# The conditioning of the first block on TensorE: plain fp32 products in four column strips in place of dot products on VectorE

## The chip, the cores and the metric

The kernel runs on one core of a Trainium2 chip, as one program with one launch. The metric is the device time of one execution in microseconds (us). The kernel before was timed three times: 2343.14 us in the median, 2342.88 to 2343.78. The profile shows one more execution of the same program. The engines are named as in the profile: PE is TensorE's matrix products, PEld its weight loads, DVE is VectorE, ACT is ScalarE, POOL is GpSimd, SP is SyncE, whose queue issues nearly all DMAs.

## The reference, cut to what matters

Two transformer blocks work on 256 tokens of width 1024. The change lies in the first of them, up to its FFN:

```python
c_act = silu(c)                                  # one row of 1024
mod = c_act @ ada_w + ada_b                      # [1024] x [1024, 6144]
sh1, sc1, g1, sh2, sc2, g2 = split(mod, 6)       # six rows of 1024
h = rmsnorm(x, mix_norm_pre) * (1 + sc1) + sh1
y = windowed_gqa_sink(h, w_qkv, w_o, ...)        # 16 q heads, 4 kv heads, 256 tokens
x = x + g1 * rmsnorm(y, mix_norm_post)
h = rmsnorm(x, ffn_norm_pre) * (1 + sc2) + sh2
y = swiglu(h, ffn_w_in, ffn_w_out)
x = x + g2 * rmsnorm(y, ffn_norm_post)
```

`mod` is called the conditioning here. It is a vector of 6144 numbers, each a dot product of 1024 terms, kept on the chip as a tile `mod1` of 128 partitions x 48 columns: column j holds outputs 128j to 128j+127. Attention needs sh1 and sc1 (columns 0 to 15) before anything else, g1 (16 to 23) at its end, sh2 and sc2 (24 to 39) ahead of the FFN, g2 (40 to 47) at the end of the FFN. The rest of the program (the FFN, the second block with its expert layers) is the same work before and after.

## The kernel before, in words

All dense weights are fp32 and are multiplied as sums of fp32r parts: `split` rounds a weight tile on ACT to `hi` (L199) and takes `lo` = raw - `hi` on DVE or on POOL (L200; the word "pool" in the weights' plan says which). A product is then three fp32r matmuls: hi x hi, hi x lo, lo x hi. Small products (attention scores, values, transposes) are plain fp32.

**The front (to the first q tile).** SP issues the loads in the order of the code: x, constants, the row c, the bias table's inputs, then the weights of the conditioning's first 16 columns (16 tiles of 512 KB, two in one DMA) with the four k/v weight slabs in between. ACT and DVE normalize x and PE transposes it into four PSUM banks (`T_half`, L389). Then comes a loop over four slabs (`kv_prep`, `kv_T`, `kv_mm`). For each, DVE makes four columns of the conditioning (`ada`, L318: a 128x1024 tile of weights times the broadcast row silu(c), summed along the row into one column of `mod1`), ACT and DVE turn two banks of transposed x into the parts `hTh` and `hTl` (L412, L417, L419), and PE multiplies them with the slab (L675 to L677). A small product (L638) selects the rows of the bias table; DVE masks it (L682), ACT's queue writes it to DRAM, and SP reads it back.

**The attention loop (`for u in range(16 + 6)`).** A step u is one half of a pair of heads. PE makes the scores of u (L732), the transposes of u-3 (L766), the values of u-4 (L779) and, in every second step, the next q tile (24 fp32r products, L223 to L225); from u = 16 on, one tile of the output projection each. DVE adds the bias and finds the maximum (L735, L738, L740), and normalizes (L755 to L757); ACT takes the exponentials (L747). A list `pending` holds generators whose pieces are spread over the loop by `pump`: here `ada` for columns 16 to 39, one or two dot products of DVE in a step. Of the 16 splits of q and output weights, 12 take their `lo` on POOL.

**Behind the loop.** The gate's row is made on PE (`row_pe`, L348), the last two tiles of the output projection follow (`gemm_tail`), `drain()` finishes what is left of the conditioning on DVE, and then DVE and ACT normalize, add to x, normalize again, PE transposes, and the FFN begins.

All engines run their own instructions strictly in the order of the code; there is no scheduler. Eight PSUM banks, five `raw` tiles for loaded weights and seven `big` tiles come from rotating pools.

Of the kernel before, what the change touches and what calls it, by code (L numbers as in the profile page):

```python
# [19 lines left out]
P = 128  # L20
# [18 lines left out]
NCOLS = 253  # L39
# [41 lines left out]
def _plan(t):  # L81

    p = [(("q", j), t["att_q"][j], "pool") for j in range(8)]
    p += [(("o", k), t["att_o"][k], ("big", "big pool")[k % 2] if k >= 8 - O_TAIL else "pool" if k % 2 else None) for k in range(8)]
# [27 lines left out]
O_TAIL = 2  # L112
# [12 lines left out]
def tile_two_blocks(ctx: ExitStack, tc: tile.TileContext, t: dict, taps=None):  # L125
# [176 lines left out]
    def ada(w, row, mod, bcol, chunks, group=8, loaded=None, also=None):  # L302
# [4 lines left out]
        for i, j in enumerate(chunks):  # L307
# [14 lines left out]
            if j % group == group - 1:  # L322
                s = slice(j - group + 1, j + 1)
                for o, c, m in todo:
                    vec.tensor_tensor(out=m[:, s], in0=m[:, s], in1=cols[:, bcol + s.start:bcol + s.stop], op=OP.add)
            yield
# [276 lines left out]
    for s in range(2):  # L603
        dma(out=X[:, s, :], in_=t["x"][s * P:s * P + P, :])
    dma(out=kst[:, 0:256], in_=t["kst"][:, 0:256])
    dma(out=crow, in_=t["c"].partition_broadcast(P))
# [3 lines left out]
    dma(out=cols[:, 0:C_AB2], in_=t["cols"][:, 0:C_AB2])  # L610
    order, early, kvw = [], [], big()
    for q in range(4):
        a = big().rearrange("p (c k) -> p c k", c=4)
        for i, j in enumerate((8 + 2 * q, 2 * q)):
            dma(out=a[:, 2 * i:2 * i + 2, :], in_=t["ada1"][j:j + 2].rearrange("c p k -> p c k"))
            order += [j, j + 1]
        early += [a[:, i, :] for i in range(4)]
        dma(out=kvw[:, q * 1024:q * 1024 + 1024], in_=t["att_kv"][q])
    W.load_to(W.used + 2)
    dma(out=sink, in_=t["sink"].partition_broadcast(P))  # L620
    mhalf = const.tile([P, 2], F32, name="mhalf")
    vec.memset(mhalf, -0.5)
    mod1 = mods[0]
    first = ada(t["ada1"], crow, mod1, C_AB1, order, 2, early)
# [4 lines left out]
    cand_c = kst[:, K_CAND:K_CAND + 32]  # L629
    bs = T_banks()  # L630
    for hf in range(2):
        rms_half(X, N, hf)
        T_half(bs, N, hf)
        if hf == 0:
            silu_row(crow)

    b = mm([P, 512])
    pe.matmul(b[0:16, :], lhsT=rb, rhs=oh[0:32, :], start=True, stop=True)  # L638
# [11 lines left out]
    def kv_prep(k2):  # L650

        j = k2 * 2
        kvs[k2] = split(kvw[:, k2 * 1024:k2 * 1024 + 1024], "pool")
        for i in range(4):
            if i == 2 and k2:
                kv_T(k2 - 1, None, vec)
                kv_mm(k2 - 1)
            next(first)
# [1133 lines left out]
```

## Time and profile before

| | |
|---|---|
| time, median of 3 runs | 2343.14 us (2342.88 to 2343.78) |
| the profiled execution's own time | 2341.82 us |
| its span | 2340.0 us |
| PE busy in the span | 2231.0 us (95%) |
| DVE busy | 1723.9 us (74%) |
| ACT busy | 1159.4 us (50%) |
| POOL busy | 223.7 us (10%) |
| DMA, mean | 227 GB/s |

The shares are means over the whole program; the change touches its first 167 us alone, up to the FFN's first product. So the rows further down are of that stretch, and of two later places where PE does what the kernel before does not do in it. A product's end is modelled in the profile: products overlap, and what one costs in a stream is read from the distance of two starts, not from its duration. "Idle before" in brackets is the engine's wait and what ended it.

### The profile page before, as it was taken

The numbers are of one execution on the slowest core, as the hardware profiler recorded it, in microseconds if no ns is written. First come the engines' busy times: TensorE is split into PE (matmuls) and PEld (weight loads), VectorE is DVE, ScalarE is ACT, GpSimd is POOL, SyncE is SP. The second block draws the span as 40 slices with busy tenths as digits, with TensorE's granted clock in tenths as the row PEclk, the third lists the DMA queues.
The fourth block names the chain that finished last, engine by engine and source line by source line (L and its number), as shares of the span: only waits on it lengthen the run. The fifth ranks groups of instructions, "written<-read, shape, count | busy, mean of one in ns | idle before, by whom it ended". The sixth has DMA issues, their size and how long they took to land. (4 is left out here: it accounts for less than half of the span.)

```text
span 2340.0 us, 36878 instructions
## 1 busy us (share of the span) xinstructions
PE 2231.0 (95%) x14334; PEld 1979.0 (85%) x14334; DVE 1723.9 (74%) x2870; ACT 1159.4 (50%) x1693; POOL 223.7 (10%) x142
## 2 busy tenths in 40 slices
PE   5979899997999999999999999999999999999998
PEld 4668888875799999998988887889999998988886
DVE  5989977727689778776787667769877746566666
ACT  4663344348555544534444445554455544444443
POOL 2234410111220000000000001230000000000001
PEclk8989999999999999999999999999999999999999
DMA  8566686730555677898899776545577777777774
GB/s 333 198 205 228 240 274 223 264 98 28 189 164 191 211 260 261 271 323 274 288 301 304 244 247 225 191 161 181 192 240 241 245 225 231 214 240 240 245 245 153
DMA packets 205023, 531.61 MB, mean 227 GB/s; under 512 B 16336, under 2 KB 84464, under 8 KB 204720
## 3 DMA queue, kind: packets, MB, share of 16 engines
q1 hardware_dynamic: 195600, 495.67, 63.6%
q10 hardware_dynamic: 9248, 33.59, 4.4%
q8 instruction: 112, 1.84, 0.3%
q14 instruction: 63, 0.52, 0.1%
HBM read 492.45 MB, written 36.75 MB: 226 GB/s over the span
## 5 line engine op out<-in xcount | busy, mean ns | idle before, releaser
L200 DVE TENSOR_TENSOR lo<-raw,hi 128x1024 fp32r<-128x1024 f32 x621 | 769.2, 1241 | 443.8 <-ACT hi L199 442.3
L199 ACT ACTIVATE hi<-raw 128x1024 fp32r<-128x1024 f32 x668 | 705.3, 1059 | 777.0 <-PE mm L244 359.7
L225 PE MATMUL mm<-hTh,lo 128*128 128x256 f32 x2592 | 739.9, 285 | 21.9 <-POOL lo L200 14.6
L223 PE MATMUL mm<-hTh,hi 128*128 128x256 f32 x2592 | 748.4, 289 | 0.7 <-ACT hTh L417 0.7
L224 PE MATMUL mm<-hTl,hi 128*128 128x256 f32 x2592 | 736.5, 284 | 0.2 <-DVE hTl L419 0.2
L225 PEld LDWEIGHTS mm<-hTh,lo 128*128 128x128 f32 x2592 | 500.1, 193 | 29.0 <-POOL lo L200 18.1
L223 PEld LDWEIGHTS mm<-hTh,hi 128*128 128x128 f32 x2592 | 500.4, 193 | 4.3 <-issue 3.0
L224 PEld LDWEIGHTS mm<-hTl,hi 128*128 128x128 f32 x2592 | 500.7, 193 | 0.7 <-POOL hTl L419 0.5
L242 PE MATMUL mm<-lo,s 128*128 128x512 f32 x992 | 305.9, 389 | 2.6 <-DVE lo L200 2.6
L240 PE MATMUL mm<-hi,s 128*128 128x512 f32 x992 | 305.6, 389 | 0.0
L244 PE MATMUL mm<-hi,s 128*128 128x512 f32 x992 | 305.5, 389 | 0.0
L200 POOL TENSOR_TENSOR lo<-raw,hi 128x1024 fp32r<-128x1024 f32 x47 | 123.0, 2619 | 1057.1 <-ACT hi L199 1035.8
L242 PEld LDWEIGHTS mm<-lo,s 128*128 128x128 f32 x992 | 186.0, 188 | 42.3 <-DVE lo L200 3.7
L244 PEld LDWEIGHTS mm<-hi,s 128*128 128x128 f32 x992 | 186.1, 188 | 39.0 <-DVE s L200 0.3
L240 PEld LDWEIGHTS mm<-hi,s 128*128 128x128 f32 x992 | 185.8, 188 | 38.4
L1424 ACT ACTIVATE t<-mm 128x512 f32<-128x512 f32 x128 | 75.7, 592 | 88.5 <-DMA gspill<-t 43.2
L318 DVE SCALAR_TENSOR_TENSOR raw<-raw,t 128x1024 f32<-128x1024 f32 x84 | 104.7, 1246 | 19.9 <-DMA raw<-in_ada_dram 15.4
L427 POOL TENSOR_TENSOR sm<-sm,mhalf 128x1 f32<-128x1 f32 (+1 forms) x18 | 11.5, 640 | 863.7 <-DVE sm L426 863.6
L1406 DVE TENSOR_TENSOR t<-t,pk 128x1024 f16<-128x1024 f16 x128 | 88.6, 692 | 4.5
L1417 PE MATMUL mm<-t 128*128 128x128 f16 x1024 | 79.7, 220 | 11.2 <-DVE t L1406 11.2
L1403 DVE TENSOR_TENSOR t<-pk,iota 128x1024 f16<-128x1024 f16 x128 | 87.7, 685 | 0.7 <-PE mm L1417 0.7
L318 DVE SCALAR_TENSOR_TENSOR raw<-raw,big 128x1024 f32<-128x1024 f32 x40 | 81.1, 2029 | 8.5 <-DMA raw<-in_ada_dram 7.7
(284 smaller groups left out, 2507.7 us busy)
## 6 DMA issues: line engine op xcount, KB each, us to landing
raw<-in_u_dram SPq DMA_DIRECT2D x256, 512.0 KB, 4.2
raw<-in_v_dram SPq DMA_DIRECT2D x256, 512.0 KB, 4.0
raw<-in_ada_dram SPq DMA_DIRECT2D x124, 512.0 KB, 4.6
gspill<-t ACTq DMA_DIRECT2D x64, 512.0 KB, 3.3
t<-gspill SPq DMA_DIRECT2D x64, 512.0 KB, 5.5
raw<-in_ffn_in_dram SPq DMA_DIRECT2D x44, 512.0 KB, 4.4
raw<-in_ab_in_dram SPq DMA_DIRECT2D x32, 512.0 KB, 4.8
raw<-in_ffn_out_dram SPq DMA_DIRECT2D x22, 512.0 KB, 4.7
```

The source lines that it names most:

```text
L199: act.activation(out=hi, in_=src, func=AF.Copy)
L200: (eng or vec).tensor_tensor(out=lo, in0=src, in1=hi.bitcast(F32), op=OP.subtract)
L223: pe.matmul(out, lhsT=sh, rhs=mh, start=(i == 0), stop=False)
L224: pe.matmul(out, lhsT=sh, rhs=ml, start=False, stop=False)
L225: pe.matmul(out, lhsT=sl, rhs=mh, start=False, stop=(i == n - 1))
L240: pe.matmul(o[c], lhsT=sh[:, tk], rhs=wh[:, cs[c]], start=first, stop=False)
L242: pe.matmul(o[c], lhsT=sh[:, tk], rhs=wl[:, cs[c]], start=False, stop=False)
L244: pe.matmul(o[c], lhsT=sl[:, tk], rhs=wh[:, cs[c]], start=False, stop=last)
L318: vec.scalar_tensor_tensor(out=o, in0=r, scalar=1.0, in1=c, op0=OP.mult, op1=OP.mult, accum_out=m[:, j:j + 1])
L1403: vec.tensor_tensor(out=o12, in0=pk[:, 0].rearrange("p a q n -> p (a q) n").unsqueeze(2).to_broadcast([P, 4, P, 2]), in1=iota2.unsqueeze(1 ...
L1406: vec.tensor_tensor(out=o[:, 1024:2048].rearrange("p (a q i n) -> p a q i n", q=2, i=P, n=2), in0=o1.to_broadcast([P, 2, 2, P, 2]), in1=pk ...
L1417: pe.matmul(b[:, n, :], lhsT=o[:, 0, a, 1, :, m], rhs=o[:, 1, a, q, :, m], start=q == 0, stop=q == 1)
```

## The change

`ada_pe` takes the place of `ada` for columns 0 to 39 of the first block's conditioning. The weights are laid out anew in DRAM (`ada1n`: ten groups of 512 outputs, each in four pieces of 128 partitions x 1024). A piece holds two slices of 128 inputs (z = 0, 1), each for 512 outputs, and the outputs in two halves of 256 (h = 0, 1). For each of the four pairs (z, h) PE does one plain fp32 product of 256 columns: the stationary operand is one column of silu(c) (a new 8-column part of `cols`) repeated 32 times, and the output goes to 32 partitions of one PSUM bank, which start at 64z + 32h. These are the four column strips. After four pieces ACT copies the bank to SBUF, and two small products with a 128x2 tile `strips` (which adds the strips of z = 0 and z = 1) turn the rows into four columns of `mod1`; DVE adds the bias. So a group is five steps of the generator. The groups 2, 0, 3, 1 are done in the front (10 steps, then 2 and 1 between the k/v products, then 7), the groups 4 to 9 in the attention loop, where `pump(1)` now stands twice in each step. The four k/v slabs are treated in two halves of two, all `lo` parts up to the last output tile are on DVE, the bias table's product and its masking stand ahead of the normalization of x, and the row c is loaded and activated later. Columns 40 to 47 stay dot products on DVE.

```diff
@@ _plan
-    p = [(("q", j), t["att_q"][j], "pool") for j in range(8)]
-    p += [(("o", k), t["att_o"][k], ("big", "big pool")[k % 2] if k >= 8 - O_TAIL else "pool" if k % 2 else None) for k in range(8)]
+    p = [(("q", j), t["att_q"][j], None) for j in range(8)]
+    p += [(("o", k), t["att_o"][k], "big" if k >= 8 - O_TAIL else None) for k in range(8)]
@@ new, behind ada
+    def ada_pe(groups, pieces=None):
+        todo = [(g, q) for g in groups for q in range(4)]
+        nxt = None if pieces else load(t["ada1n"][todo[0]])
+        for i, (g, q) in enumerate(todo):
+            if pieces:
+                r = pieces[i]
+            else:
+                r = nxt
+                nxt = load(t["ada1n"][todo[i + 1]]) if i + 1 < len(todo) else None
+            r = r.rearrange("p (z h n) -> p z h n", z=2, h=2)
+            if q == 0:
+                b = mm([P, 512])
+            for z in range(2):
+                c = cols[:, C_CC + 2 * q + z:C_CC + 2 * q + z + 1].to_broadcast([P, 32])
+                for h in range(2):
+                    o = 64 * z + 32 * h
+                    pe.matmul(b[o:o + 32, 0:256], lhsT=c, rhs=r[:, z, h, :], start=q == 0, stop=q == 3)
+            if q < 3:
+                yield
+                continue
+            f = s1(256)
+            act.activation(out=f, in_=b[:, 0:256], func=AF.Copy)
+            yield
+            o = b[:, 256:260].rearrange("p (h a) -> p h a", a=2)
+            for a in range(2):
+                pe.matmul(o[:, :, a], lhsT=f[:, a * P:a * P + P], rhs=strips, start=True, stop=True)
+            vec.tensor_tensor(out=mods[0][:, g * 4:g * 4 + 4], in0=b[:, 256:260],
+                              in1=cols[:, C_AB1 + g * 4:C_AB1 + g * 4 + 4], op=OP.add)
+            yield
@@ the front: loads, then the bias table ahead of the normalization of x
-    dma(out=crow, in_=t["c"].partition_broadcast(P))
+    dma(out=cols[:, 0:C_AB2], in_=t["cols"][:, 0:C_AB2])
+    dma(out=cols[:, C_CC:NCOLS], in_=t["cols"][:, C_CC:NCOLS])
...
+    early, kvw = [], big()
+    for i, g in enumerate((2, 0, 3, 1)):
         a = big().rearrange("p (c k) -> p c k", c=4)
+        for q in range(4):
+            dma(out=a[:, q, :], in_=t["ada1n"][g, q])
+            early.append(a[:, q, :])
+        if i % 2:
+            for q in range(i - 1, i + 1):
+                dma(out=kvw[:, q * 1024:q * 1024 + 1024], in_=t["att_kv"][q])
...
-    first = ada(t["ada1"], crow, mod1, C_AB1, order, 2, early)
+    act.activation(out=cols[:, C_CC:NCOLS], in_=cols[:, C_CC:NCOLS], func=AF.Silu)
...
+    strips = const.tile([P, 2], F32, name="strips")
+    vec.tensor_tensor(out=strips, in0=ident[:, 0:64:32], in1=ident[:, 64:128:32], op=OP.add)
+    first = ada_pe((2, 0, 3, 1), early)
     bs = T_banks()
+    b = mm([P, 512])
+    pe.matmul(b[0:16, :], lhsT=rb, rhs=oh[0:32, :], start=True, stop=True)
+    vec.tensor_tensor(out=msk[0:16, :], in0=b[0:16, :], in1=msk[0:16, :], op=OP.add)
+    adma(out=btab, in_=msk[0:16, :])
     for hf in range(2):
         rms_half(X, N, hf)
         T_half(bs, N, hf)
-        if hf == 0:
-            silu_row(crow)
-    b = mm([P, 512])
-    pe.matmul(b[0:16, :], lhsT=rb, rhs=oh[0:32, :], start=True, stop=True)
@@ the front: conditioning and k/v slabs
-    for k2 in range(4):
-        kv_prep(k2)
...
+    for part in range(2):
+        ada_steps(10 if part == 0 else 7)
+        j = part * 4
+        vec.scalar_tensor_tensor(out=s1c[:, j:j + 4], in0=mod1[:, 8 + j:12 + j], scalar=1.0,
+                                 in1=cols[:, C_MPRE + j:C_MPRE + j + 4], op0=OP.add, op1=OP.mult)
+        for k2 in range(part * 2, part * 2 + 2):
+            kvs[k2] = split(kvw[:, k2 * 1024:k2 * 1024 + 1024], None)
+            kv_T(k2)
+        for k2 in range(part * 2, part * 2 + 2):
+            if part == 0:
+                ada_steps(2 - k2)
+            kv_mm(k2)
+    silu_row(crow)
@@ the attention loop
-    pending.append(ada(t["ada1"], crow, mod1, C_AB1, range(16, 36)))
+    pending.append(ada_pe(range(4, 10)))
...
-        if u == 10:
-            late = big().rearrange("p (c k) -> p c k", c=4)
-            dma(out=late[:, 0:4, :], in_=t["ada1"][36:40].rearrange("c p k -> p c k"))
-            pending.append(ada(t["ada1"], crow, mod1, C_AB1, range(36, 40), loaded=[late[:, i, :] for i in range(4)]))
...
         W.ahead(2 if u % 2 else 0)
+        pump(1)
...
-        pump((u > 1) + (u > 16))
+        pump(1)
```

On ACT the program begins as follows before (`s_147` and `s_149` are scratch of the sums of squares of x's first half, `t_104` is the row c):

```order
L433 ACT_TABLE_LOAD
L433 ACTIVATE s_147,sm<-big 128x512
L433 ACTIVATE s_149,sm<-big 128x512
L442 ACTIVATE big<-big,sm 128x512
L329 ACT_TABLE_LOAD
L329 ACTIVATE t_104<-t_104 128x1024
```

and after (L466 and L475 are what L433 and L442 were, `cols` the eight columns of c, `t_108` the masked bias table):

```order
L659 ACT_TABLE_LOAD
L659 ACTIVATE cols<-cols 128x8
L674 DMA btab<-t_108 16x512
L466 ACTIVATE s_163,sm<-big 128x512
L466 ACTIVATE s_165,sm<-big 128x512
L475 ACTIVATE big<-big,sm 128x512
```

The sums of squares have moved behind the issue of the table's DMA, which waits for the masking on DVE and by it for the table's product on PE.

On PE two steps of the attention loop between two q tiles read so before (L732 scores, L766 transposes, L779 values):

```order
L732 MATMUL mm_688<-big_189 128x256 x2
L766 MATMUL mm_704<-kst_100,s1_539 128x128 x4
L779 MATMUL mm_647<-big_380,big_189 64x256 x2
L732 MATMUL mm_724<-big_189 128x256 x2
L766 MATMUL mm_736<-kst_100,s1_596 128x128 x4
L779 MATMUL mm_742<-big_380,big_189 64x256 x2
```

and after (L766 scores, L800 transposes, L813 values, L347 the strips' products, L356 the products with `strips`):

```order
L356 MATMUL mm_600<-strips_152,s1_669 128x2 x2
L766 MATMUL mm_718<-big_202 128x256 x2
L347 MATMUL mm_736<-raw_663,cols_99 32x256 x4
L800 MATMUL mm_741<-kst_100,s1_558 128x128 x4
L813 MATMUL mm_677<-big_454,big_202 64x256 x2
L347 MATMUL mm_736<-raw_734,cols_99 32x256 x4
L766 MATMUL mm_764<-big_202 128x256 x2
L347 MATMUL mm_736<-raw_753,cols_99 32x256 x4
L800 MATMUL mm_782<-kst_100,s1_613 128x128 x4
L813 MATMUL mm_788<-big_454,big_202 64x256 x2
```

A piece of four strip products stands on PE between scores and transposes, and another behind the values; the dot products that stood on DVE between maximum and normalization are gone.

## Rows read from the trace of the kernel before

**Rows 1.** Busy time by stretch: length; PE, PEld, DVE, ACT, POOL; PE clock, DMA, GB/s.
```profile
20.00:50.00 30.00, 20.73 (x49) 13.72 (x50) 24.34 (x42) 14.22 (x29) 11.54 (x5) 0.77 1.01 387
50.00:125.00 75.00, 67.78 (x380) 49.22 (x379) 64.62 (x141) 47.39 (x130) 18.45 (x8) 0.98 0.58 190
125.00:147.00 22.00, 22.00 (x106) 16.77 (x105) 17.32 (x30) 10.35 (x18) 6.15 (x3) 1.00 0.74 241
```
**Rows 2.** Timeline of the front: start, duration (us), engine, line, operation.
```profile
4.48 0.63 ACT L433 ACTIVATE s<-big 128x512 f32<-128x512 f32 x1 [2.46 <-DMA big<-in_x_dram]
...
7.41 1.28 ACT L329 ACT_TABLE_LOAD   x1
...
14.53 1.89 PE L638 MATMUL mm<-t,rb 32*16 32x512 f32 x2
...
27.18 0.67 DVE L682 TENSOR_TENSOR t<-mm,t 16x512 f32<-16x512 f32 x1
...
40.10 3.38 DVE L318 SCALAR_TENSOR_TENSOR big<-big,t 128x1024 f32<-128x1024 f32 x1
...
43.60 0.15 DVE L659 SCALAR_TENSOR_TENSOR s1c<-mod,cols 128x2 f32<-128x2 f32 x1
...
49.98 0.28 PE L223 MATMUL mm<-hTh,hi 128*128 128x256 f32 x1
```
**Rows 3.** Groups of instructions from 0 to 50 us: busy us, mean ns.
```profile
L318 DVE SCALAR_TENSOR_TENSOR big<-big,t 128x1024 f32<-128x1024 f32 x16 | 25.4, 1623 | 0.0
...
L412 ACT ACTIVATE s<-mm,mod,s1c 128x128 f32<-128x128 f32 x16 | 6.4, 449 | 17.2 <-DVE s1c L659 11.8 <-DVE t L682 5.4
...
L199 ACT ACTIVATE hi<-big 128x1024 fp32r<-128x1024 f32 x4 | 4.2, 1049 | 2.9 <-DMA big<-in_att_kv_dram 2.9
...
L419 DVE TENSOR_TENSOR hTl<-s,hTh 128x256 fp32r<-128x256 f32 x8 | 3.2, 421 | 2.1 <-ACT hTh L417 2.0
```
**Rows 4.** Timeline of two steps of the attention loop.
```profile
75.24 1.22 DVE L318 SCALAR_TENSOR_TENSOR raw<-raw,t 128x1024 f32<-128x1024 f32 x1
...
75.56 1.13 PE L732 MATMUL mm<-big 64*128 64x256 f32 x4
...
76.61 0.66 PE L766 MATMUL mm<-kst,s 128*128 128x128 f32 x4
...
77.20 1.08 PE L779 MATMUL mm<-big 128*64 128x256 f32 x4
...
78.37 2.35 POOL L200 TENSOR_TENSOR lo<-raw,hi 128x1024 fp32r<-128x1024 f32 x1 [6.50 <-ACT hi L199]
78.55 2.20 DVE L740 TENSOR_SCALAR sm<-sm,sink 128x2 f32<-128x2 f32 x1
```
**Rows 5.** Timeline: the gate's row on PE, and what follows it there.
```profile
145.41 1.95 PE L348 MATMUL mm<-kst,c 128*128 128x128 f32 x16
...
147.12 0.48 PE L267 MATMUL mm<-big 128*128 128x512 f32 x1
```
**Rows 6.** Timeline in the second block: two fp32 products, one on each half of the rows.
```profile
510.35 1.13 PE L1105 MATMUL mm<-big 64*128 64x512 f32 x4
511.41 0.50 PE L985 MATMUL mm<-hi,hTh 128*128 128x512 f32 x1
```
**Rows 7.** Timeline inside a q tile: weight loads beside products.
```profile
50.10 0.28 PE L224 MATMUL mm<-hTl,hi 128*128 128x256 f32 x1
50.11 0.19 PEld L225 LDWEIGHTS mm<-hTh,lo 128*128 128x128 f32 x1
...
50.23 0.28 PE L225 MATMUL mm<-hTh,lo 128*128 128x256 f32 x1
```
**Rows 8.** Timeline behind the attention loop.
```profile
149.70 3.42 DVE L318 SCALAR_TENSOR_TENSOR big<-big,t 128x1024 f32<-128x1024 f32 x1
...
150.89 0.60 ACT L433 ACTIVATE s<-mm 128x512 f32<-128x512 f32 x1 [0.70 <-PE mm L269]
...
154.39 0.15 DVE L435 SCALAR_TENSOR_TENSOR sm<-sm 128x1 f32<-128x1 f32 x1
```

More of the change, by code (lines that the diff above doesn't have):

```diff
@@ L38 @@
 C_DNG, C_SGUB, C_PSC = 240, 241, 245
-NCOLS = 253
+C_CC = 253
+NCOLS = C_CC + 8
 K_ID, K_REV, K_COS, K_SIN, K_CAND = 0, 128, 256, 384, 512
@@ L609, in tile_two_blocks @@
     dma(out=msk[0:16, :], in_=t["relhot"][32:48, :])
-    dma(out=cols[:, 0:C_AB2], in_=t["cols"][:, 0:C_AB2])
-    order, early, kvw = [], [], big()
-    for q in range(4):
+    early, kvw = [], big()
+    for i, g in enumerate((2, 0, 3, 1)):
         a = big().rearrange("p (c k) -> p c k", c=4)
[L614 to L618, printed above, removed]
+        for q in range(4):
[4 more added lines that the diff above has]
+                dma(out=kvw[:, q * 1024:q * 1024 + 1024], in_=t["att_kv"][q])
     W.load_to(W.used + 2)
     dma(out=sink, in_=t["sink"].partition_broadcast(P))
+    dma(out=crow, in_=t["c"].partition_broadcast(P))
     mhalf = const.tile([P, 2], F32, name="mhalf")
@@ L648, in tile_two_blocks, with kv_T @@
     kvs, fs = {}, {}
[L650 to L658, printed above, removed]
-        vec.scalar_tensor_tensor(out=s1c[:, j:j + 2], in0=mod1[:, 8 + j:10 + j], scalar=1.0,
-                                 in1=cols[:, C_MPRE + j:C_MPRE + j + 2], op0=OP.add, op1=OP.mult)
-    def kv_T(k2, eng, lo):
-        if eng:
-            fs[k2] = s1(512)
+    def kv_T(k2):
+        fs[k2] = s1(512)
         for hf in range(2):
-            T_part(bs, fs, k2, hf, s1c, mod1[:, 0:8], hT, eng, eng, lo)
+            T_part(bs, fs, k2, hf, s1c, mod1[:, 0:8], hT, vec if hf else act, act, vec)
     def kv_mm(k2):
@@ L677, in kv_mm, with ada_steps @@
                 pe.matmul(acc[hf], lhsT=hT[1][:, k, tk], rhs=wh[:, w], start=False, stop=(k == 7))
-    for k2 in range(4):
-        kv_prep(k2)
-        if k2 == 1:
-            vec.tensor_tensor(out=msk[0:16, :], in0=b[0:16, :], in1=msk[0:16, :], op=OP.add)
-            adma(out=btab, in_=msk[0:16, :])
-        kv_T(k2, act, None)
-    W.ahead(0)
-    kv_T(3, None, vec)
+    def ada_steps(n):
+        for _ in range(n):
+            next(first)
+    for part in range(2):
[11 more added lines that the diff above has]
+    silu_row(crow)
     W.ahead(2)
-    kv_mm(3)
     dma(out=kst[:, 256:], in_=t["kst"][:, 256:])
-    dma(out=cols[:, C_AB2:], in_=t["cols"][:, C_AB2:])
+    dma(out=cols[:, C_AB2:C_CC], in_=t["cols"][:, C_AB2:C_CC])
     biases = [big()[:, 0:8 * 384].rearrange("p (h k) -> p h k", k=384) for _ in range(2)]
@@ L1747, in _layout @@
         [colv(i[k]) for k in ("mix_norm_pre", "mix_norm_post", "ffn_norm_pre", "ffn_norm_post", "ada_b", "ada_b_2",
-                              "ln_g_2", "ln_b_2", "diff_norm_g_2", "sgu_b_2", "pool_scale_2")], axis=1)
+                              "ln_g_2", "ln_b_2", "diff_norm_g_2", "sgu_b_2", "pool_scale_2", "c")], axis=1)
     out["rel_bias"] = i["rel_bias"]
@@ L1751, in _layout @@
     out["ada1"] = i["ada_w"][0].T.reshape(48, P, D)
+    out["ada1n"] = i["ada_w"][0][:, :5120].reshape(4, 2, P, 10, 512).transpose(3, 0, 2, 1, 4).reshape(10, 4, P, 1024)
     out["ada2"] = i["ada_w_2"].transpose(0, 2, 1).reshape(2, 48, P, D)
```

## The prediction

> **What bounds the kernel now.** Only the stretch up to the FFN changes, so I first cut it by the windows [rows 1], then read the timeline of each stage, then looked elsewhere in the trace for operations like the new ones. The reader should see three stages.
>
> The front, to the first q tile at 49.98 [rows 2]. Sixteen dot products take DVE 25.4 us [rows 3], some of them 3.38 instead of about 1.2 where a POOL split runs beside them [rows 2]; DVE is busy 24.34 of the 30 us from 20 to 50 [rows 1]. PE and ACT wait for it: the group L412 stood idle 11.8 us for the scale that DVE makes behind its dot products [rows 3]. The loads run at 387 GB/s in that time, the most of any stretch [rows 1], so they are a second bound not far below.
>
> The attention loop. DVE is busy 64.62 of 75 us, and PE 67.78; from 125 to 147 PE is busy 22.00 of 22.00 [rows 1]. So the two engines are nearly level, and PE has 75 - 67.78 = 7.2 us of idle time from 50 to 147, no more. That number decides.
>
> Behind the loop DVE is late: it still does dot products at 149.70, each 3.42 long, while ACT has the second sum of squares done at about 151.6 (150.89 + 0.60); DVE takes it up at 154.39 [rows 8].
>
> **The change part by part.**
>
> *One piece on PE.* Two fp32 products of 256 columns on the same rows cost 76.61 - 75.56 = 1.05 us from start to next start, 0.53 each [rows 4]. Whether four strips of columns run side by side no row shows. The nearest: two products of 512 columns on two halves of the rows took 511.41 - 510.35 = 1.06 [rows 6]. In line, at twice 1.05 for twice the columns, they would have taken about 2.1; so halves of the rows do run side by side. I carry this over to strips of columns: four products in the time of one, 0.53. Then the change of shape: four transposes between scores and values take 77.20 - 76.61 = 0.59 [rows 4], while products of that size follow each other at (147.12 - 145.41)/16 = 0.107 [rows 5], 0.43 for four. So a change costs about 0.16, and each piece brings one more than the loop had: 0.53 + 0.16 = 0.69. From both sides: 0.43 if all of it streams and no change costs anything; 4 x 0.53 = 2.1 in line. I take 0.69, by the row nearest in kind [rows 6].
>
> A rule speaks against the pieces here. The Trainium skill, "TensorEngine Tiling (Array Packing)", Key Properties, says that a change of tiling mode drains TensorE. The trace agrees that a change costs something, and puts it at 0.16 us. Without the rule the 24 pieces of the loop would be 3.8 us cheaper.
>
> *One `strips` step.* Two plain fp32 products with a full stationary tile each, seen as four passes of 0.107 [rows 5] and a change: 0.6.
>
> *The attention loop.* 24 pieces x 0.69 = 16.6, six `strips` steps x 0.6 = 3.6: 20 us more on PE. What leaves is DVE's: 20 dot products of 1.22 [rows 4] and the stalls beside POOL (a 128x2 operation of 2.20 [rows 4]), against 12 more `lo` parts of about 1.2 on DVE. That frees DVE, but PE is the longer one already, so it only gives back PE's waits: of 7.2 us I count 6. New waits: a `strips` step waits for ACT's copy, which stands behind two exponentials in ACT's queue, and behind it on PE stand transposes and values; and a piece waits for its tile, since with two of five `raw` tiles held for the q weights only one is loaded ahead. I put 3 us on both (0 to 6). Sum: 20 - 6 + 3 = +17. The moved `lo` parts and the bias additions cost nothing while DVE has this slack.
>
> *The front.* The sums of squares of x, now at 4.48, stand behind the table's DMA on ACT. The table's inputs are loaded right behind x and the columns, landing at about 7; then the product 1.89, masking 0.67 [rows 2] and the issue: squares at about 10.2, 5.7 later. Transposes end at 14.53 now, where L638 follows them [rows 2]; ACT's activation of c leaves that chain with its table load of 1.28 [rows 2], about 2.3 together: they end at 18, and PE, in order, begins its pieces there. The first eight have landed by then (1.3 MB and eight tiles at 387 GB/s: about 17). PE comes out of idle time, so I count four pieces at 1.4, at the lower clock, four at 0.69, and 1.5 for the `strips` step between, which waits for ACT: 18 + 9.9 = 27.9. Copy, `strips` step, addition and scale: 1.9, so the first scale is there at 29.8.
>
> Two slabs of k/v in one go: DVE has 2 x (1.2 + 0.42 + 0.7 + 0.42) = 5.5, waits for ACT's rounding (1.05), scaling (0.9) and `hTh` (as long as `hTl`, 0.42) in between [rows 3], and seven products follow: 9.5. Now one slab takes 49.98 - 43.60 = 6.4 [rows 2]. Then five pieces and a `strips` step, 5.0, again 1.9, again 9.5: 29.8 + 9.5 + 5.0 + 1.9 + 9.5 = 55.7, against 49.98: +6. From both sides: the last early tile lands at about 30 (10.8 MB), and 1.9 + 9.5 + 3 for what is not hidden end at 44 at the earliest: -6; with all pieces at the lower clock, +11. I take +6, the chain, because nothing in the code overlaps its parts.
>
> *Behind the loop.* All pieces are done by u = 14, so DVE takes up the squares at 151.7 instead of 154.39: -2.7, and PE's wait for a POOL part goes: -3. What comes next is the second half's sum of squares, bounded by PE.
>
> Sum: +6 + 17 - 3 = +20 on 2341.8, the profiled execution's own time: 2362. The median of the runs is 1.3 us above that execution; 2362 is my forecast for the changed kernel's median too, within the rounding of the terms.
>
> **The rivals.**
>
> *The strips run in line.* For: no row of this kernel has two products on different columns; side by side they need four streams from the same rows, whereas the halves of rows 6 need one stream per row. Then a piece costs 2.1, 1.4 more: 24 x 1.4 = 34 in the loop and 13 x 1.4 = 18 in the front, so about 2414; half in line, 2388. Against: rows 6. The Trainium skill, "TensorE: Matmul & The Clock Gate", Part 3, says weight loads overlap products in flight only when the row groups differ; strips share all rows, so by it loads and products would alternate and this rival's time would follow. The trace does not agree with the rule so put: a load at 50.11, on all rows, lasts 0.19 beside the product of 50.10, and the next product starts at 50.23 [rows 7].
>
> *The front ends at the loads (faster).* If the two slabs' conversions overlap with pieces and products, the front ends near 44 (-6). With pieces at their lower bound the loop gives 24 x 0.43 + 6 x 0.43 - 7.2 = +6, the end -4 to -5: about 2337. For: DVE's 25.4 us are the front's largest item, and they go. Against: both ends are bounds, not expectations. It decides faster from 0.45 us per piece downward, and only together with a front at the loads.
>
> *Even.* The chain of the front as now (49 to 51), pieces at 0.55, all waits given back: 0 + 24 x 0.55 + 3 - 7.2 = +9, -4 behind the loop, and 2 to 4 us back because PE stays at its higher clock (the granted clock is 0.77 from 20 to 50 [rows 1]): about 2344.
>
> **How the numbers follow.** The forecast, strips side by side and PE as bound, has 0.62, with its own range 2350 to 2374. In line or partly so: 0.15. Front at the loads: 0.13. Even: 0.10. So 2362, and the range goes from 2338, which leaves out most of the faster case, to 2398, which takes in half-in-line strips but not the full 2414. A measurement here can tell about 0.2%, 4.7 us, from no change: faster 0.14, within it 0.10, slower 0.76.
>
> **What would show it.** Each step can be read off the changed profile. Strips: four starts within hundredths of a microsecond, and a piece of about 0.7 from its first start to the next instruction. The loop: PE with hardly any idle time from the first q tile to the gate's row, that stretch about 17 us longer than 97, DVE well under three quarters busy. The front: squares on ACT near 10, first strip product near 18, first q tile near 56. The end: L435's successor about 1 us behind the squares. I would be wrong if the first q tile came before 50, if a piece cost under 0.45, or if PE's busy time in the loop held work that was not there without DVE's waits.

## The result and the profile after

| | before | after |
|---|---|---|
| time, median of the runs on one chip | 2343.01 us | 2359.12 us |
| ratio, with its 95% interval | | 1.0068 [1.0053, 1.0083] |
| the profiled execution's own time | 2341.82 us | 2355.99 us |
| its span | 2340.0 us | 2354.2 us |
| PE busy in the span | 2231.0 us | 2255.3 us |
| DVE busy | 1723.9 us | 1674.2 us |

The changed kernel is slower by 0.68%, 16 us; 2362 was forecast. First the windows of the changed kernel, which answer to [rows 1] (same columns):

```profile
20.00:50.00 30.00, 24.34 (x177) 15.10 (x170) 12.83 (x28) 14.49 (x27) 0.00 (x0) 0.89 1.03 393
50.00:125.00 75.00, 67.61 (x466) 46.42 (x464) 34.57 (x91) 38.35 (x99) 0.00 (x0) 0.91 0.55 184
125.00:147.00 22.00, 20.34 (x134) 12.27 (x133) 13.47 (x40) 13.81 (x41) 0.00 (x0) 1.00 0.63 204
```

DVE has gone from 64.62 to 34.57 us in the first 75 us of the loop. PE is no busier there than before, 67.61 against 67.78, though 19 of the 24 pieces fall into this window (152 of their records, eight each), so less of the loop's other work fits in: PE stands still for 7.4 us, as long as before, and its clock is 0.91 instead of 0.98. So PE's own work isn't all that sets the length of this stage.

The timeline of the changed kernel's front, which answers to [rows 2]:

```profile
10.10 0.35 ACTq L674 DMA_DIRECT2D btab<-t  x1
10.49 0.63 ACT L466 ACTIVATE s<-big 128x512 f32<-128x512 f32 x1 [3.56 <-DVE t L673]
...
18.18 3.64 PE L347 MATMUL mm<-big,cols 128*32 128x256 f32 x32
22.32 0.61 PE L356 MATMUL mm<-strips,s 128*128 128x2 f32 x4 [0.50 <-ACT s L352]
22.86 1.93 PE L347 MATMUL mm<-big,cols 128*32 128x256 f32 x32
...
26.15 0.15 DVE L712 SCALAR_TENSOR_TENSOR s1c<-mod,cols 128x4 f32<-128x4 f32 x1
...
40.07 0.15 DVE L712 SCALAR_TENSOR_TENSOR s1c<-mod,cols 128x4 f32<-128x4 f32 x1
...
50.87 0.28 PE L224 MATMUL mm<-hTh,hi 128*128 128x256 f32 x1
```

L347 are the strip products (32 records for a group of four pieces, two for each product), L356 the `strips` step, L712 the scale. The squares come at 10.49, six us later than before, the first strip product at 18.18; the first q tile at 50.87, 0.9 us behind the kernel before.

The loop as one window each, from the first q tile to the gate's row, the kernel before:

```profile
49.98:145.41 95.43, 88.20 (x469) 64.42 (x468) 80.35 (x169) 56.76 (x146) 23.59 (x10) 0.98 0.61 199
```

and the changed kernel, with the two stretches of it in which the clock is at its lower level:

```profile
50.87:168.01 117.14, 108.09 (x685) 73.69 (x684) 56.03 (x142) 60.68 (x153) 0.00 (x0) 0.94 0.55 180
...
66.33:76.57 10.24, 9.53 (x44) 7.61 (x48) 2.32 (x8) 2.19 (x8) 0.00 (x0) 0.50 0.43 153
83.40:86.81 3.41, 3.33 (x15) 1.66 (x16) 0.73 (x2) 1.55 (x5) 0.00 (x0) 0.50 0.87 263
```

The loop is 21.7 us longer: PE's busy time grows by 19.9, its idle time from 7.23 to 9.05. All of the idle time has one cause, in the list of PE's waits (us in total, times, longest) from 50 to 170:

```profile
PE mm L347 <- DMA raw<-in_ada1n_dram: 9.1, 7, 4.5
```

and the DMA queue's own waits in the same stretch say what held those loads back:

```profile
SPq L196 <- PE mm L347: 48.4, 19, 8.2
SPq L196 <- DVE sm L790: 20.7, 6, 9.5
```

A load (L196) waits on SP for PE to be done with an earlier piece, or for DVE, and SP issues its loads in order. Ahead of PE's longest wait, a load of q weights stands for 4.3 us until the split on DVE (L201) ends at 62.02; the next piece's load stands behind it, is issued at 62.48 and lands at 67.00. PE stands still, and the half clock (0.50 in the windows above) follows: one piece's timeline shows both, 4.51 us of waiting and 1.08 us for eight records that take 0.64 otherwise.

```profile
60.27 0.64 PE L347 MATMUL mm<-raw,cols 128*32 128x256 f32 x8
60.84 1.13 PE L766 MATMUL mm<-big 64*128 64x256 f32 x4
61.90 0.64 PE L347 MATMUL mm<-raw,cols 128*32 128x256 f32 x8
67.04 1.08 PE L347 MATMUL mm<-raw,cols 128*32 128x256 f32 x8 [4.51 <-DMA raw<-in_ada1n_dram]
```

Behind the loop, answering to [rows 5, 8], the gate's row, the second sum of squares, its successor on DVE, and the FFN's first product:

```profile
168.01 1.95 PE L381 MATMUL mm<-kst,c 128*128 128x128 f32 x16
...
172.75 0.60 ACT L466 ACTIVATE s<-mm 128x512 f32<-128x512 f32 x1 [0.63 <-PE mm L270]
...
173.47 0.55 DVE L468 SCALAR_TENSOR_TENSOR sm<-sm 128x1 f32<-128x1 f32 x1 [9.69 <-ACT s L466]
...
185.70 0.58 PE L224 MATMUL mm<-hTh,hi 128*128 128x256 f32 x1 [0.66 <-ACT hTh L450]
```

DVE now waits for ACT's second sum, where it came 2.9 us late to it before (154.39 against 150.89 + 0.60). From the gate's row to the FFN it is 17.69 us, against 20.81 (145.41 to 166.22).

So the FFN starts 19.5 us later, and the span is only 14.2 us longer. Most of the other 5.3 us comes from one later stretch, which the change doesn't touch. Between the first f16 product of the first product-key stage and a later q tile the two programs have the same instructions, 246.2 us of them in the kernel before:

```profile
779.88 0.52 PE L1417 MATMUL mm<-t 128*128 128x128 f16 x6
...
1026.09 0.28 PE L223 MATMUL mm<-hTh,hi 128*128 128x256 f32 x1
```

and 241.4 in the changed one:

```profile
799.44 0.57 PE L1448 MATMUL mm<-t 128*128 128x128 f16 x7
...
1040.80 0.28 PE L224 MATMUL mm<-hTh,hi 128*128 128x256 f32 x1
```

In the 14 executions of this study that were profiled this stretch takes 238.7 to 246.2 us, the one of the kernel before the longest. I put that down to the difference from one execution to the next; with one profile of each kernel it isn't shown. That is why the experiments are read from their stages up to the FFN, with the times of many runs beside them.

### The profile page after: what moved, and what is told of

Its sections match the earlier page's. It is cut to its first block, busy times and chain, and to the rows that moved or that the text cites. A ratio compares the mean times of both kernels' runs of the same rounds, so it can differ in the third digit from the quotient of the medians.

```text
span 2354.2 us, 37537 instructions
## 1 busy us (share of the span) xinstructions
PE 2255.3 (96%) x14694; PEld 1989.1 (84%) x14694; DVE 1674.2 (71%) x2812; ACT 1159.4 (49%) x1695; POOL 182.7 (8%) x126
## 5 line engine op out<-in xcount | busy, mean ns | idle before, releaser
L201 DVE TENSOR_TENSOR lo<-raw,hi 128x1024 fp32r<-128x1024 f32 x632 | 783.1, 1241 | 450.7 <-ACT hi L200 444.3
L226 PE MATMUL mm<-hTh,lo 128*128 128x256 f32 x2592 | 738.6, 285 | 21.5 <-POOL lo L201 15.1
L201 POOL TENSOR_TENSOR lo<-raw,hi 128x1024 fp32r<-128x1024 f32 x36 | 96.6, 2683 | 1135.8 <-ACT hi L200 1123.6
L319 DVE SCALAR_TENSOR_TENSOR raw<-raw,t 128x1024 f32<-128x1024 f32 x64 | 78.1, 1221 | 16.1 <-DMA raw<-in_ada_dram 11.9
L201 DVE TENSOR_TENSOR s<-big,s 128x512 fp32r<-128x512 f32 x126 | 86.2, 684 | 0.0
```

Source lines behind the costliest of these rows:

```text
L201: (eng or vec).tensor_tensor(out=lo, in0=src, in1=hi.bitcast(F32), op=OP.subtract)
L226: pe.matmul(out, lhsT=sl, rhs=mh, start=False, stop=(i == n - 1))
L319: vec.scalar_tensor_tensor(out=o, in0=r, scalar=1.0, in1=c, op0=OP.mult, op1=OP.mult, accum_out=m[:, j:j + 1])
```

## The experiments

Three starts are read from each trace: the first q tile, the gate's row, the FFN's first product. "Front", "loop" and "tail" are the stretches that they end. The ratio is to runs of the kernel before on the same chip (medians 2340.6 to 2343.0), with its 95% interval.

| kernel | median us | ratio | front | loop | tail | FFN at |
|---|---|---|---|---|---|---|
| before | | | 49.98 | 95.4 | 20.8 | 166.2 |
| changed | 2359.1 | 1.0068 [1.0053, 1.0083] | 50.87 | 117.1 | 17.7 | 185.7 |
| dot products back in the loop | 2341.0 | 0.9991 [0.9979, 1.0003] | 49.17 | 98.9 | 19.0 | 167.1 |
| no loads of pieces | 2344.1 | 1.0006 [0.9995, 1.0016] | 49.08 | 103.4 | 17.7 | 170.2 |
| half the pieces on one strip | 2361.1 | 1.0074 [1.0053, 1.0095] | 48.69 | 121.0 | 17.7 | 187.4 |
| pieces in tiles of their own | 2343.5 | 1.0013 [0.9999, 1.0028] | 50.37 | 106.2 | 17.7 | 174.3 |
| squares first | 2353.5 | 1.0063 [1.0050, 1.0076] | 48.79 | 116.8 | 17.7 | 183.3 |
| mixture | 2337.7 | 0.9994 [0.9984, 1.0004] | 49.43 | 97.4 | 20.7 | 167.6 |
| mixture, last group in the gap | 2337.7 | 0.9994 [0.9984, 1.0004] | 49.78 | 97.8 | 17.6 | 165.2 |
| mixture, no GpSimd splits | 2337.6 | 0.9987 [0.9975, 0.9999] | 47.52 | 92.9 | 21.2 | 161.7 |
| before, no GpSimd splits | 2338.5 | 0.9986 [0.9975, 0.9998] | 49.89 | 92.0 | 21.2 | 163.1 |
| both of these edits, silu later | 2333.0 | 0.9957 [0.9942, 0.9971] | 49.72 | 94.5 | 17.6 | 161.9 |
| both of these edits | 2333.2 | 0.9964 [0.9952, 0.9976] | 49.91 | 94.9 | 17.6 | 162.5 |
| the same, PE kept busy in the front | 2330.6 | 0.9956 [0.9941, 0.9970] | 44.96 | 93.3 | 17.6 | 155.9 |

The theory after the first comparison: the front is even, and the loop loses by two things, PE's work for the pieces and the waits for their loads. The rival: the waits stand only where PE would wait anyway, or the loss comes from the front.

### Dot products back in the loop

```diff
-    pending.append(ada_pe(range(4, 10)))
+    pending.append(ada(t["ada1"], crow, mod1, C_AB1, range(16, 36)))
...
+        if u == 10:
+            late = big().rearrange("p (c k) -> p c k", c=4)
+            dma(out=late[:, 0:4, :], in_=t["ada1"][36:40].rearrange("c p k -> p c k"))
+            pending.append(ada(t["ada1"], crow, mod1, C_AB1, range(36, 40), loaded=[late[:, i, :] for i in range(4)]))
```

> The first four groups of the conditioning stay column-strip products (the front of the changed kernel); groups 4 to 9 are dot products on DVE inside the attention loop again, and the weight splits on GpSimd are back. Theory A (the loss is made in the attention loop: 20 us of TensorE work for the pieces and 9 us of waits for their loads; the front is even): the first q tile at 50.9 us as in the changed kernel, the gate's row 95.4 us behind it as in the kernel before, so 2343 + 0.9 = 2344 us (2341 to 2348). Theory B (a good part of the loss comes from the front or from what the front leaves behind, such as the later transfers): 2350 us or more.

2340.96 us, no difference from the kernel before that can be measured; the FFN starts 0.9 us later than there. Theory A held: the whole loss is made in the loop, and the column strips in the front, by themselves, neither win nor lose. The GpSimd splits came back in the same run; what they do by themselves is tried further down.

### No loads of pieces

```diff
-    pending.append(ada_pe(range(4, 10)))
+    once = [load(t["ada1n"][4, 0])] * 24
+    pending.append(ada_pe(range(4, 10), once))
```

> Leaves out the loads of the loop's pieces: all 24 pieces of groups 4 to 9 are one tile that is loaded once, so their values are wrong and every product, copy and strip step is still made. Theory A (the 9.05 us in which TensorE waits for a piece's load are time lost, and the half-clock stretches that follow the pauses, 13.7 us against 3.4 before, cost about 3 us more): 9 to 12 us less than the changed kernel, 2347 to 2350 us, with no wait of L347 for a transfer left and about 12 us of loss that is the products' own. Theory B (the piece waits only stand where TensorE would wait for DVE or ACT anyway, as it does for 7.2 us in the kernel before): 7 us of idle time come back under other names and the run is at 2355 to 2358 us.

2344.06 us, 15 less than the changed kernel, more than either theory said. Its loop as one window:

```profile
49.08:152.51 103.43, 102.04 (x685) 69.96 (x684) 57.23 (x143) 61.12 (x154) 0.00 (x0) 1.00 0.29 90
```

PE is idle for 1.39 us and never leaves the full clock. With the same 685 records PE is busy for 102.04 us instead of 108.09: 6.05 us of the changed kernel's busy time were the half clock, twice the 3 that theory A allowed. The loop splits up: the products' own work 102.04 - 88.20 = 13.84; the idle time of the kernel before, -7.23; the waits for loads, +9.05; the half clock, +6.05. Sum 21.71, as measured; the parts are taken from the same windows, so the sum has to come out. The loop of the kernel before has one stretch at the half clock as well, 3.41 us long, worth about 1.7 (an estimate, half its length), so the products' own work is nearer 15.5 than 13.84. 13.7 of the 21.71 (117.14 - 103.43) went with the loads. Theory B fell: the 7 us did not come back under other names.

### Half the pieces on one strip

```diff
-                    o = 64 * z + 32 * h
+                    o = 64 * z + 32 * h if pieces or q in (0, 3) else 0
```

> In the attention loop, two of the four pieces of each group (12 of 24) put all four of their products on the first column strip instead of one on each, so their values are wrong; the count and shape of the products stay. Theory A (four strips run side by side, a round of four in 0.216 us): four products one behind the other take 8 x 0.216 = 1.73 us instead of 0.43, so 12 x 1.3 = 15.5 us more, 2374 us, less what the waits for loads give back (up to 5 us, since a slower TensorE comes later to the next piece): 2369 to 2375 us. Theory B (starts 7 ns apart are only the issue, and the products share the array's time in either case): no change, 2359 us.

2361.09 us, between the two, so the time alone says nothing. The timeline does: a piece on one strip and one on four, each with what follows it.

```profile
58.10 1.91 PE L347 MATMUL mm<-raw,cols 128*32 128x256 f32 x8
59.94 1.13 PE L766 MATMUL mm<-big 64*128 64x256 f32 x4
...
64.83 0.64 PE L347 MATMUL mm<-raw,cols 128*32 128x256 f32 x8 [1.92 <-DMA raw<-in_ada1n_dram]
65.40 0.91 PE L766 MATMUL mm<-big 64*128 64x256 f32 x3
```

From start to next start a piece takes 1.84 us in line and 0.57 side by side. So theory A is right on the strips, 12 x 1.27 = 15.2 us more work, and the loop still got only 3.8 us longer (120.98 - 117.15). The window shows where the rest went:

```profile
48.69:169.67 120.98, 118.89 (x686) 79.02 (x685) 56.73 (x142) 59.96 (x153) 0.00 (x0) 0.99 0.54 179
```

Idle time is 2.09 instead of 9.05, and the clock 0.99 instead of 0.94: PE came later to each load and hardly waited. I had allowed 5 us for that; it was 7.0 of waits and about 4 of clock. Where an engine waits for transfers, its own work can grow for nothing until the waits are used up.

### Pieces in tiles of their own

```diff
-        nxt = None if pieces else load(t["ada1n"][todo[0]])
+        def own(src):
+            r = t4()
+            dma(out=r, in_=src)
+            return r
+
+        nxt = None if pieces else [own(t["ada1n"][x]) for x in todo[0:2]]
...
-                r = nxt
-                nxt = load(t["ada1n"][todo[i + 1]]) if i + 1 < len(todo) else None
+                r = nxt.pop(0)
+                if i + 2 < len(todo):
+                    nxt.append(own(t["ada1n"][todo[i + 2]]))
```

> The loop's pieces are loaded into three t4 tiles of their own, two pieces ahead, instead of into the five raw tiles that they share with the q and o weights, one ahead. Theory A (the waits come from the shared tiles: a piece's load can't be issued before a raw tile is free and its predecessor has been consumed): most of the 9.05 us goes, and the clock with it, 2348 to 2352 us. Theory B (the waits come from the transfers themselves or from loads behind one another on SP's queue): under 3 us is saved, 2356 to 2360 us, and the waits move to the weights or stay.

2343.51 us, better than theory A's best: all loads are there, and in time the loss to the kernel before is gone within what can be measured. The loop, and the one stretch of it at the half clock:

```profile
50.37:156.58 106.21, 104.86 (x686) 72.59 (x685) 56.60 (x142) 60.90 (x153) 0.00 (x0) 0.97 0.58 196
64.96:71.79 6.83, 6.83 (x36) 6.14 (x36) 2.64 (x10) 2.35 (x8) 0.00 (x0) 0.50 0.51 195
```

1.35 us idle, and that is a `strips` step waiting for ACT's copy, not for a load; the half clock follows it:

```profile
64.89 0.98 PE L363 MATMUL mm<-strips,s 128*128 128x2 f32 x4 [1.35 <-ACT s L359]
```

The run without loads has the same wait, 1.4 us, and no half clock behind it. So the transfers themselves were in time at 196 GB/s; what held them was the tile that each had to wait for. The two edits to the buffers and to the depth go together here; which of them does it was not tried apart. Up to the FFN this kernel is still 8 us behind the kernel before, which is the products' work and the half clock, less the tail's gain. Why the times are equal all the same is not shown: in this profile the later stretch with the same instructions takes 238.8 us, in that of the kernel before 246.2, and no other execution of either was profiled.

### Squares first

```diff
+    for hf in range(2):
+        rms_half(X, N, hf)
+        T_half(bs, N, hf)
     b = mm([P, 512])
...
     adma(out=btab, in_=msk[0:16, :])
-    for hf in range(2):
-        rms_half(X, N, hf)
-        T_half(bs, N, hf)
```

> The changed kernel, with the bias table's product, its mask and its transfer put behind the two transposes of the normalized x instead of ahead of its squares. Theory A (the front is held by the late squares, 10.5 us against 4.5 before, and gets the pieces by then): the squares come 5.7 us earlier, the first scale goes from 26.2 to 21 us (piece 8 has landed at about 20 us, the group's tail takes 1.5), the second from 40.1 to about 35 (its last piece lands at about 33), and the first q tile is at 45 to 47 us; 4 to 6 us less than the changed kernel, 2353 to 2355 us. Theory B (the front is bound by its transfers: everything that the first q tile needs has to come in at 1.28 us for 512 KB): the second scale stays near 40 us and the run within 1.5 us of the changed kernel, 2358 to 2359 us.

2353.54 us, in theory A's range; but the kernel before takes 2340.6 on the chip of this run, against 2343.0 on the one from which the range was reckoned. By the ratios, 1.0063 against 1.0068, whose intervals overlap, no gain is shown. The front gave 2.1 us: the first scale at 24.05 and the second at 37.98, neither theory's number. The squares start at 6.59, behind the silu of the new column, which waits for its load until 6.48. The bias table's product now stands between the transposes and the strip products:

```profile
14.26 1.88 PE L675 MATMUL mm<-t,rb 32*16 32x512 f32 x2
```

And PE works at the half clock up to about 20 us (the first group takes 3.64 us, the second 1.93).

### The mixture, and the last group in the gap

The mixture is the two kernels above in one: squares first, dot products and GpSimd splits in the loop. The second kernel makes the last four pieces with column strips behind the loop:

```diff
+            dma(out=late[:, 0:4, :], in_=t["ada1n"][9].rearrange("c p k -> p c k"))
+            last = ada_pe((9,), [late[:, i, :] for i in range(4)])
...
     rms_residual(y1, X, 1)
+    for _ in last:
+        pass
+    s2c, b2c = fold(mod1[:, 32:40], mod1[:, 24:32], cols[:, C_FPRE:C_FPRE + 8])
```

> The order of the run before (squares first) together with DVE dot products and GpSimd splits in the attention loop. Theory A (front and loop add up): 4 to 6 us less than the kernel with the dot products in the loop alone (2341), so 2335 to 2337 us, faster than the kernel before. Theory B (the front is bound by transfers, or the loop waits for its first weights and biases anyway): 2340 to 2342 us.

> As the mixture of early squares and DVE dot products in the loop, but the last group (four pieces) as column-strip products in the 6.8 us in which TensorE stands still behind the loop. Theory A (the dot products queued on DVE behind the loop, two of 3.4 us, hold the statistics of the rows; the strip products fit in TensorE's gap): 2 to 3 us less than the mixture. Theory B (the gap is filled at the price of the chain, the ACT copy and the strips step of the last group come late): no gain, or up to 2 us more than the mixture.

2337.69 and 2337.74 us, both with an interval that takes in no change, the first between the two theories' ranges. By the stages, the mixture's front is at 49.43, no better than with the dot products in the loop alone: theory B. The edit behind the loop does shorten its stretch by 3.1 us, from 20.7 to 17.6, and by the FFN the kernel is 2.4 us ahead; the times don't show it, so theory A is borne out by the trace alone.

### No GpSimd splits

> The mixture (early squares, DVE dot products in the loop) with all weight splits up to the FFN on DVE, none on GpSimd. Theory A (a split on GpSimd holds DVE's instructions that start beside it: the 128x2 TENSOR_SCALAR of the maxima takes 0.88 us in the mean and a dot product up to 3.4; so the 12 splits more on DVE, 14.6 us, are about paid by what the others get shorter): within 2 us of the mixture. Theory B (DVE, 64.6 us busy of 75 in the first part of the loop, gets the bound): 5 to 12 us more than the mixture.

> The kernel before, with one part of the change alone: the splits of the q and o weights are on DVE, none of them on GpSimd; the four splits of the k and v weights stay on GpSimd, and the whole conditioning stays dot products on DVE. Theory A (the GpSimd splits cost more by what they hold on DVE than they save; taking them off shortened the loop of the mixture from 97.4 to 92.9 us): the loop goes from 95.4 to 91 to 93 us and the run 2 to 5 us below the kernel before, 2338 to 2341 us. Theory B (DVE with the whole conditioning in the front has no room for them, 24.3 of 30 us busy between 20 and 50 us): 3 to 10 us above the kernel before.

The plan of the changed kernel (`None` for the q and o weights) in the mixture, and alone in the kernel before: 2337.60 and 2338.51 us, the second 0.14% below the kernel before. Theory A of both held in the stages: the loop goes from 97.4 to 92.9 us, and from 95.4 to 92.0. Two groups on DVE from 50 to 140 us (busy us, mean ns), in the mixture:

```profile
L319 DVE SCALAR_TENSOR_TENSOR raw<-raw,t 128x1024 f32<-128x1024 f32 x18 | 24.1, 1338 | 2.6 <-DMA raw<-in_ada_dram 2.6
L774 DVE TENSOR_SCALAR sm<-sm,sink 128x2 f32<-128x2 f32 x16 | 14.1, 882 | 0.6
...
L201 DVE TENSOR_TENSOR lo<-raw,hi 128x1024 fp32r<-128x1024 f32 x3 | 3.7, 1218 | 1.0 <-ACT hi L200 1.0
```

and without the GpSimd splits:

```profile
L319 DVE SCALAR_TENSOR_TENSOR raw<-raw,t 128x1024 f32<-128x1024 f32 x20 | 24.4, 1218 | 2.4 <-DMA raw<-in_ada_dram 2.4
L201 DVE TENSOR_TENSOR lo<-raw,hi 128x1024 fp32r<-128x1024 f32 x12 | 14.7, 1222 | 5.2 <-ACT hi L200 5.0 <-issue 0.3
...
L774 DVE TENSOR_SCALAR sm<-sm,sink 128x2 f32<-128x2 f32 x16 | 3.7, 229 | 0.6
```

The splits cost DVE 11.0 us more (14.7 - 3.7), and the tiny operation on the maxima, on which every exponential waits, gives back 10.4, the dot products 0.12 each. DVE is about as busy as before, and its chain is shorter. The Trainium skill, "SBUF — State Buffer", section "SBUF: two separate sides", has DVE and GpSimd share one pair of ports under an exclusive lock: a GpSimd operation, or a DVE operation in a mode that takes two ports or with two inputs in SBUF, holds it for the whole instruction. The trace agrees, with 0.88 us in the mean against 0.23 for the same 128x2 operation; in which mode that operation runs no run shows.

### Put together

> Column strips in the front (squares ahead of the silu and of the bias table, pieces of the fourth group placed between the k and v products), dot products on DVE in the loop, no GpSimd splits, and the last group as column strips in TensorE's gap behind the loop. Theory A (the places add up): first q tile at 44 to 46 us (47.5 in the mixture with all splits on DVE), loop 93 us, 17.6 us from the gate's row to the FFN (21.2 there), so the FFN starts at 154.5 to 157 us against 166.2 in the kernel before, and the run takes 2331 to 2334 us. Theory B (the front is at its transfers' end, or the tail's gain is taken by the chain as it was in the times of the mixture with that edit): FFN at 158 us or later, 2336 to 2339 us.

> The mixture with all splits on DVE (early squares, dot products on DVE in the loop), and the last group's four pieces as column strips in TensorE's gap behind the loop. Theory A (both add up): loop 93 us as in that mixture, 17.6 us from the gate's row to the FFN (21.2 without the edit), the FFN at 158 us, 2332 to 2335 us. Theory B (with the last group's loads in the loop the splits on DVE come late): loop 95 us or more and FFN at 160 us or later.

> The same, and with four products of a tile of zeros on TensorE from the first microsecond, two more behind the second scale, and the bias table's product between the two halves of the transposes; nothing reads what the six products write. Theory A (the front is held by the half clock, 1.2 GHz up to 20 to 25 us, since TensorE stands still up to 9.6 us and between the halves): the clock rises between 9 and 16 us, the first group takes 1.9 instead of 3.6 us and the transposes 1 instead of 2, the first scale is at 21.5 to 22.5 us (its last piece lands at 20) instead of 24 to 26.5, and without the half-clock stretch at 41 us the first q tile is at 44 to 46 us; 2 to 4 us less than without, 2329 to 2332 us. Theory B (the front is at its transfers' end): the clock rises earlier and the first scale stays at 24 us or later, no gain.

The last of the three adds to the second:

```diff
+    warm = s1(512)
+    vec.memset(warm, 0.0)
+
+    def warm_up(n):
+        wb = mm([P, 512])
+        for _ in range(n):
+            pe.matmul(wb, lhsT=warm[:, 0:P], rhs=warm, start=True, stop=True)
+
+    warm_up(4)
...
+        if part:
+            warm_up(2)
```

All three beat both kernels, the kernel before by about 0.4%. With the silu later, and pieces between the k and v products, the time is in theory A's range, but the front (49.72) is not, the loop at 94.5 was 1.5 us longer than I wrote, and the FFN at 161.9 is theory B's. Whether that order gains anything can't be told: in its profile the first two groups both ran at the half clock, 3.64 us each. The second gave 2333.21, A's range; its loop, at 94.9, and the FFN at 162.5, are B's. The third has the lowest median of the study, 2330.60 us; by its ratio, 0.9956 [0.9941, 0.9970], it is level with the first, 0.9957, which ran on another chip. The second and the third on one chip: the front without the six products of zeros,

```profile
9.79 1.97 PE L422 MATMUL mm<-kst,big 128*128 128x128 f32 x8 [9.79 <-ACT big L475]
...
16.31 3.64 PE L347 MATMUL mm<-big,cols 128*32 128x256 f32 x32
...
21.40 3.52 PE L347 MATMUL mm<-big,cols 128*32 128x256 f32 x32
...
26.28 0.15 DVE L712 SCALAR_TENSOR_TENSOR s1c<-mod,cols 128x4 f32<-128x4 f32 x1
```

and with them:

```profile
1.48 5.12 PE L664 MATMUL mm<-s 128*128 128x512 f32 x8 [1.48 <-DVE s L659]
...
9.41 1.09 PE L422 MATMUL mm<-kst,big 128*128 128x128 f32 x8 [2.81 <-ACT big L475]
...
14.11 3.64 PE L347 MATMUL mm<-big,cols 128*32 128x256 f32 x32
...
18.85 1.93 PE L347 MATMUL mm<-big,cols 128*32 128x256 f32 x32
...
22.14 0.15 DVE L722 SCALAR_TENSOR_TENSOR s1c<-mod,cols 128x4 f32<-128x4 f32 x1
```

The first scale comes 4.1 us earlier, the first q tile at 44.96 instead of 49.91: theory A. One of its steps failed. The clock rose at 4.4 us, but PE stood still for 2.8 us before the transposes and it fell again, so the first group is still at the half clock:

```profile
4.40:11.20 6.80, 3.99 (x16) 1.61 (x14) 0.97 (x4) 3.38 (x10) 0.91 (x2) 1.00 1.00 317
11.20:18.00 6.80, 5.93 (x41) 2.96 (x40) 1.07 (x2) 0.84 (x2) 0.20 (x1) 0.50 1.02 416
18.00:44.96 26.96, 22.76 (x165) 13.51 (x166) 11.78 (x27) 13.80 (x27) 0.00 (x0) 1.00 1.04 398
```

How much of the 4.95 us is the zeros and how much the bias table's product, which moved between the halves, was not tried apart; and some of it may be the difference between executions, since the mixture without GpSimd splits, with the same front as the second kernel, had its first q tile at 47.52. The gain in time over the second kernel, 2.6 us, is smaller than the front's, and the intervals overlap.

## Why the prediction was right, and where its terms were not

Direction and size were right: +20 forecast, +16 measured, the FFN 19.5 us later. Three of its terms were wrong, and their errors cancel, so it is in part luck that the sum comes so near. That the loop loses, by PE's work for the pieces and by waits for their loads, was in the prediction.

**Strips side by side: right.** 32 records of four strips take 1.93 us, eight in line 1.91. The rival "in line" is out; a group would have cost four times as much. The Trainium skill, "TensorE: Matmul & The Clock Gate", Part 3, lists a packing of three column strips as 2.38 times as fast as without; the trace agrees in kind, with 1.84 / 0.57 = 3.2 times for a piece on four strips. It does not agree with the rule on row groups in the same part as I used it for this rival.

**The price of a piece: too high.** 0.69 was 0.53 and 0.16 for a change of shape. A piece takes 0.57 (60.27 to 60.84), and two in a row take 1.00 us (60.41 to 61.41) in the run without loads, so 0.43 for the one more:

```profile
60.41 1.07 PE L347 MATMUL mm<-raw,cols 128*32 128x256 f32 x16
61.41 1.13 PE L767 MATMUL mm<-big 64*128 64x256 f32 x4
```

The row from which 0.53 came [rows 4] ran from the first score to the first transpose, so it had a change in it already, and I added it once more. All work on PE was 13.8 us by the windows, about 15.5 with both kernels at the full clock, not 20.

**Waits given back: right; new waits: the term that failed.** Of 7.2 us I counted 6 as given back; the run without loads gave back all but 1.4. But "3 us on both (0 to 6)" for new waits became 9.05 us of standing still and 6.05 of half clock behind it, 15.1. The mechanism stood in the prediction, only one tile loaded ahead with two of five held for the q weights. Its price was a guess, without a row, and without the clock. "PE with hardly any idle time" in the loop was wrong: it stood still for 9.05 us, all of it for loads. The other wait of that term, a `strips` step for ACT's copy, shows only where the loads' waits are gone, once, with 1.4 us.

**The front: +6 forecast, +0.9.** Squares near 10, first strip product near 18: right (10.49, 18.18). Then each piece was cheaper: four at the half clock took 3.64 us with their change, not 5.6, four at the full clock 1.93, not 2.8, and the first scale came at 26.15 instead of 29.8. From there to the second scale it is 13.9 us against 16.4 in the sum, and behind the second scale 10.8 against 9.5, 6.8 of it at the lower clock. The front is a chain, as I had it, with terms too long.

**Behind the loop: -3, and -3.1 measured.** DVE takes up the second sum at 173.47, right behind ACT's 172.75 + 0.60, as written. The run with the last group in the gap shows the same 3.1 us in a kernel that keeps its dot products in the loop.

**Of the rivals** "even" was the nearest to what the strips can do. It had 0.55 a piece, the front's chain as before and all waits given back, and said 2344. The kernel with tiles of its own for the pieces is at 2343.5. That it meets the number is in part luck: its loop is 10.8 us longer where "even" had 9, the clock gave nothing back, and at the FFN it is 8 us behind where "even" had about 2. What kept the changed kernel from it were 13.7 us that went with the loads, which had no price in any rival.

## What to carry to other kernels

When work moves from one engine to another, count its loads as well as its instructions: the consumer's order decides when their tiles come free, and a load that is late costs the wait and then, here, the lower clock. An engine that is busy beside a longer one is no reason to move its work; here taking 12 splits off GpSimd shortened the loop by 3.4 to 4.5 us, and taking 24 dot products off DVE lengthened it, by 21.7 us, and still by 10.8 with the waits for loads gone. And read the price of an operation between two starts of the same kind, or you pay the change of shape twice.

## What the runs showed of the hardware

Four fp32 products of 256 columns, with 32 stationary columns each, on four column strips of the array and the same rows take 0.43 us in a stream at the full clock; four in line take 1.84, with the change to the next shape in it. A change between such products and those of another shape costs about 0.14 us (0.57 - 0.43).

The clock level in the front is not the same in each execution of nearly the same code: with the same order up to the first scale, that scale came at 24.17 in one profiled kernel of the mixture, at 25.88 and 26.14 in two others, as the second group ran at the full clock or not (1.93 against 3.31 and 3.54 us). A gain of 2 us in such a stretch can't be told from that with one profile.
